# First inputs gathered in the router, down biases added in the last sums, the modulation product summed on VectorE

## The chip, the core and the metric

The kernel runs on one core of a Trainium2 chip. The metric is the device time of one execution, in microseconds (us). Matrix products run on TensorE (PE in the rows, its weight loads PEld), elementwise work on VectorE (DVE), ScalarE (ACT) and GpSimd (POOL); SyncE (SP) issues most DMAs, in its own order. Every engine works through its instructions in order.

## What is computed

512 tokens of width 1024 pass two layers of a first block (a gated linear recurrence, retention, spatial gating, a gated projection), then a second block: attention and a short convolution, both modulated, and a mixture of experts.

```
mod = silu(c) @ w_ada + b_ada            # 1024 -> 6 x 1024; a second row of it for the context
x = x + gt1 * (concat(attention, conv) @ w_out)
h2 = rmsnorm(x) * g_norm2 * (1 + sc2) + sh2
logits = h2 @ w_router + b_router        # 32 experts, the best 4 of each token, softmax gates
for each expert e, over its tokens:
    y = swiglu(h2[tok] @ w_gate_up[e] + b_gate_up[e]) @ w_down[e] + b_down[e]
    x[tok] += gt2 * gate * y
out = rmsnorm(x) * g_final
```

All data are float32. An expert's weights are 12 MB, all experts' 403 MB.

## The kernel before

**Dense stage** (`layer`, `block2`). Activations lie transposed, eight tiles `self.h` of 128 x 512. A weight is loaded into one of three buffers of the pool `wst` (tag `w`), split into a high part `wh` on ScalarE (L289) and a rest `wl` on VectorE (L290), and multiplied in three products (L284 to L286) of 128x128 by 128x512 into one of three PSUM banks `prj`. Up to three split weights are kept ready (`weights`, `next_weights`).

**Modulation** (`ada`, L773). 24 calls are strewn over the output projections, four in a stage of eight projections, after projections 0, 1, 4 and 5. A call loads two tiles `wa` of 512 KB into two of the same three `w` buffers. TensorE multiplies them by `sc`, the two conditioning columns padded to 32, in four products (L796), each in its own 32 columns of the array; every second call ScalarE copies the sum (L801), four small products with selector columns (L805) add up the four parts and turn them, and VectorE adds the bias (L807). Only the first eight calls hold columns that the context row needs.

**Router** (`router`, L1031). Beside the last output projection it turns `h` into rows `hr` (token by token), forms scaled rows `raw` (128 x 4 x 256, four of them, two in `wst` and two in the pool `late`) on GpSimd, logits, the four best experts (`mask`), the position `pos` of each token in its expert's list, and gates `G` into `vals`. Then `raw` is scaled by the norm and shifted: number 0 on ScalarE and GpSimd, 1 to 3 on VectorE (L1155), and stored by SP as `h_rows` (L1156), from which later experts gather tokens.

**Experts** (`moe`, L1757). `ORDER` lists two wide experts (0 and 1, 128 slots each), then narrow ones (64 slots, two weights halves at once in the array, L1588) and wide ones (L1549, L1550, down L1627) in turn. Weights stream through eight buffers of 1 MB in SP's order; a wide expert's are split on ScalarE and VectorE first (L289, L290). Experts 0 and 1 take their tokens by a product of `hr` with one-hot matrices `hots` (`first_slots`, `first_inputs`, L1428); the others by an indirect DMA from `h_rows` into `xg` or `xgn` (`slots`, L1502) and four transposes (L1518). Each expert's rows are added to `x_rows` in DRAM by an indirect DMA with an add (L1231).

Work beside an expert's products is a generator `work()`, one step per call of `fill`, four in each `gate_up`, two in `down`; what is left runs at the expert's end. From the second expert on each engine's order is the program's; before that a list scheduler orders by priority, and `high_priority(n)` moves an instruction ahead by n. `issue_after` and `behind` put an instruction behind another one in its engine's queue. In expert 0 the steps are: inputs of expert 1, `ranks` (the order of the experts by size), `slots(0, 0)` (indices and gates of 0 and 1) and `slots` of the first narrow pair; `slots` of the first wide pair comes in expert 1.

`residual` (L1310), in expert 0, forms down biases times gates: the bias tile `bst`, scaled on GpSimd and split into `gb`, the gates turned into `gT` (L1330), eight products (L1336), eight adds into `hr` (L1338), four stores to `x_rows` (L1339). `narrow_consts` copies positions and gates into `pg` for the picks of later slots (L1453). `expert_bias` splits the gate and up biases, the rest on VectorE (L1754). At the end the last two experts' rows are not added in DRAM: `finish_part` multiplies them by one-hot `to` into banks `fx` (L1690) and adds these to rows read back from `x_rows`.

## Time and profile before

| | |
|---|---|
| median of 3 runs | 2409.7 us (2406.43 to 2410.49) |
| the profiled execution | 2409.16 us, of which the span is 2407.0 us |
| TensorE busy | 2286.2 us, 95% of the span |
| VectorE busy | 1589.7 us, 66% |
| ScalarE busy | 982.7 us, 41% |
| GpSimd busy | 163.1 us, 7% |
| granted TensorE clock, mean | 0.986 of full speed |
| bytes moved by DMA | 563.59 MB, mean 234 GB/s |

The span has two parts: the dense stage and the router up to about 1265 us, and the experts after it. A busy share is an average over both and says little of either; the rows below are taken by stage.

### The profile page before, as it was taken

What the parts mean: (1) busy time and instruction counts of PE and PEld (TensorE: products, weight loads), DVE (VectorE), ACT (ScalarE), POOL (GpSimd) and SP (SyncE); (2) the same over time, 40 slices, a digit from 0 to 9 for tenths busy, and PEclk for the clock granted to TensorE, in tenths of its full rate; (3) what the DMA queues carried; (4) which work ended last, traced back from release to release, by engine and by line L of the source; (5) the groups of instructions that cost most, each with busy time, mean ns of one, the idle gap of its engine ahead of it and who ended that gap; (6) DMA issues with size and microseconds to landing.
All of it is one profiled execution on the core that took longest, in us unless ns stands there. A gap on an engine that the chain in (4) does not pass through costs nothing.

```text
span 2407.0 us, 29051 instructions
## 1 busy us (share of the span) xinstructions
PE 2286.2 (95%) x10863; PEld 1639.9 (68%) x10863; DVE 1589.7 (66%) x2487; ACT 982.7 (41%) x1166; POOL 163.1 (7%) x116
## 2 busy tenths in 40 slices
PE   8999999999999999999998789999999999999995
PEld 6778877777878878788876555555566555555552
DVE  8875764768747657786768856656666565656552
ACT  5632332435423324433455434334444443444421
POOL 0000000000000000000011111011111011011002
PEclk9999999999999999999998899999999999999998
DMA  4234334332342353422126689999999999999995
GB/s 163 86 112 122 99 117 129 125 118 86 94 151 88 99 164 109 142 74 83 55 88 236 251 337 401 407 395 403 395 401 392 403 397 400 403 396 404 412 399 227
DMA packets 109282, 563.59 MB, mean 234 GB/s; under 512 B 14440, under 2 KB 16872, under 8 KB 59984
## 3 DMA queue, kind: packets, MB, share of 16 engines
q1 hardware_dynamic: 95184, 532.33, 58.2%
q0 software_dynamic: 9200, 21.00, 3.2%
q10 hardware_dynamic: 4752, 8.36, 1.1%
q8 instruction: 87, 1.43, 0.2%
q14 instruction: 59, 0.48, 0.1%
HBM read 550.73 MB, written 18.87 MB: 237 GB/s over the span
## 4 chain that ended last, share of the span: by engine, by line
PE 81%; DMA 8%; DVE 7%; ACT 3%; issue 1%; POOL 0%; DVEq 0%; SPq 0%; ACTq 0%; POOLq 0%
PE prj L284 11%; PE prj L285 11%; PE prj L286 11%; PE pg L1549 7%; PE pd L1627 7%; PE pl L1550 7%; DMA w<-in_wgu 6%; PE pd L1650 4%; DVE wl L290 3%; PE pg L1588 2%; PE pl L1588 2%; ACT wh L289 2%; PE ada L796 1%; DMA w<-in_wdn 1%; PE cs L313 1%
## 5 line engine op out<-in xcount | busy, mean ns | idle before, releaser
L289 ACT ACTIVATE wh<-w 128x2048 fp32r<-128x2048 f32 (+3 forms) x382 | 560.4, 1469 | 587.2 <-PE prj L285 197.2
L290 DVE TENSOR_TENSOR wl<-w,wh 128x2048 fp32r<-128x2048 f32 (+3 forms) x382 | 660.2, 1734 | 205.3 <-ACT wh L289 204.8
L284 PE MATMUL prj<-ty,wh 128*128 128x512 f32 x880 | 353.0, 401 | 11.3 <-ACT wh L289 8.5
L285 PE MATMUL prj<-ty,wh 128*128 128x512 f32 x880 | 350.4, 398 | 1.2 <-DVE ty L823 0.9
L286 PE MATMUL prj<-ty,wl 128*128 128x512 f32 x880 | 349.7, 398 | 1.1 <-DVE wl L290 1.1
L1588 PE MATMUL pg<-w,xn 128*64 128x512 f32 x512 | 190.0, 600 | 39.4 <-DMA w<-in_wgu 39.3
L1549 PE MATMUL pg<-wh,x 128*128 128x512 f32 x512 | 210.1, 410 | 0.6 <-ACT wh L289 0.6
L1550 PE MATMUL pl<-wh,x 128*128 128x512 f32 x512 | 203.8, 398 | 0.0
L284 PEld LDWEIGHTS prj<-ty,wh 128*128 128x128 f32 x880 | 166.5, 189 | 50.4 <-ACT wh L289 10.6
L286 PEld LDWEIGHTS prj<-ty,wl 128*128 128x128 f32 x880 | 166.2, 189 | 41.1 <-DVE wl L290 2.4
L1569 DVE TENSOR_SCALAR li<-pl 128x512 f32<-128x512 f32 x48 | 33.0, 687 | 243.0 <-PE pl L1593 242.5
L285 PEld LDWEIGHTS prj<-ty,wh 128*128 128x128 f32 x880 | 166.4, 189 | 39.2 <-DVE ty L823 1.8
L1588 PE MATMUL pl<-w,xn 128*64 128x512 f32 x512 | 185.5, 595 | 0.0
L1568 ACT ACTIVATE sg<-pg 128x512 f32<-128x512 f32 x48 | 28.7, 597 | 308.6 <-PE pg L1593 260.8
L1588 PEld LDWEIGHTS pg<-w,xn 128*64 128x64 f32 x512 | 50.2, 136 | 125.2 <-DMA w<-in_wgu 69.7
L284 PE MATMUL prj<-tmix,wh 128*128 128x512 f32 x320 | 126.9, 398 | 0.3
L285 PE MATMUL prj<-tmix,wh 128*128 128x512 f32 x320 | 126.5, 395 | 0.0
L286 PE MATMUL prj<-tmix,wl 128*128 128x512 f32 x320 | 126.2, 395 | 0.0
L1650 PE MATMUL pd<-w,an 128*64 128x512 f32 x512 | 114.8, 596 | 7.6 <-DMA w<-in_wdn 6.1
L1549 PEld LDWEIGHTS pg<-wh,x 128*128 128x128 f32 x512 | 97.1, 190 | 32.5 <-issue 11.4
L1550 PEld LDWEIGHTS pl<-wh,x 128*128 128x128 f32 x512 | 97.3, 190 | 19.3
L1549 PE MATMUL pg<-wl,x 128*128 128x512 f32 x256 | 101.6, 397 | 0.4 <-DVE wl L290 0.4
(498 smaller groups left out, 3864.9 us busy)
## 6 DMA issues: line engine op xcount, KB each, us to landing
w<-in_wgu SPq DMA_DIRECT2D x256, 1024.0 KB, 12.6
w<-in_wdn SPq DMA_DIRECT2D x128, 1024.0 KB, 10.9
w<-in_w SPq DMA_DIRECT2D x118, 512.0 KB, 3.7
wa<-in_wada SPq DMA_DIRECT2D x48, 512.0 KB, 3.6
w<-in_wob SPq DMA_DIRECT2D x32, 384.0 KB, 3.1
w<-in_wg SPq DMA_DIRECT2D x16, 512.0 KB, 3.7
w<-in_wos SPq DMA_DIRECT2D x8, 512.0 KB, 3.6
w<-in_wo SPq DMA_DIRECT2D x8, 512.0 KB, 3.5
```

The source lines that it names most:

```text
L284: mm(ps, a[0], b[0], start=first, stop=False)
L285: mm(ps, a[0], b[1], start=False, stop=False)
L286: mm(ps, a[1], b[0], start=False, stop=last)
L289: ins = self.nc.scalar.activation(hi, src, AF.Copy).ins
L290: self.nc.vector.tensor_sub(lo, src, hi.bitcast(F32))
L1549: nc.tensor.matmul(pg, x[k], w[:, s, 0], start=first, stop=False)
L1550: nc.tensor.matmul(pl, x[k], w[:, s, 1], start=first, stop=False)
L1568: nc.scalar.activation(sg, pg, AF.Sigmoid, scale=1.702)
L1569: nc.vector.tensor_scalar(li, pl, 8.0, -6.0, op0=OP.min, op1=OP.max)
L1588: nc.tensor.matmul(p[64 * c:64 * c + 64], x[k], ws[c][:, s, h], start=k == 0, stop=False, skip_group_check=True)
L1627: nc.tensor.matmul(self.pd[n], a[:, k], w[:, s, n * 512:(n + 1) * 512], start=hf == 0 and k == 0 and a is ah and w is wh, stop=hf == 1 and ...
L1650: nc.tensor.matmul(pd[64 * n:64 * n + 64], a[:, k % 4, k // 4 * 64:k // 4 * 64 + 64], w[:, s, n * 512:(n + 1) * 512], start=k == 0, stop=k ...
```

## The change

- `ada`: the `wa` tiles stay as they are. VectorE multiplies each 512-column piece by the conditioning value of its partition and adds it to an accumulator of 128 x 512 (`adac`, and `rt` for the context row in the first eight calls), eight pieces to a sum; TensorE adds up the partitions by products with a column of ones. The padded `sc`, the ScalarE copy, the selector products and `onesm` go.
- `first_slots` and the first expert's `first_inputs` move into `router`, ahead of gates and counts, with banks of `prj` and a buffer of `mix`. `ranks` moves ahead of expert 0.
- `raw` 1 to 3 are scaled on ScalarE and shifted on GpSimd as 0 was; 2 and 3 queue behind the first expert's second input split on ScalarE. `hr` is stored to `x_rows` once, in the router.
- Slots of the first narrow and the first wide pair are both steps of expert 0; `slots(0, 0)` is one of expert 1.
- `residual` becomes `down_bias`, formed in the sixth expert of `ORDER`; its eight products start the sums in `finish_part`. The path for crowded experts, which does not run here, gets its own.
- `narrow_consts` and `pg` go: picks read `pos` and `vals` in three multiplications. The rest of the gate and up biases is formed on GpSimd.
- Pads shift the start of tiles that hold rows (`hr`, `xg`, `ye`, weights).

```
@@ ada
-            self.sc = self.small.tile([128, 8, 32], F32, name="sc", bufs=1)
+            self.sc = self.small.tile([128, 16], F32, name="sc", bufs=1)
+            self.adac = self.small.tile([128, T], F32, name="adac", bufs=1)
...
+        accs = [self.adac, self.rt][:2 if u < 4 else 1]
         for t in range(2):
             w = self.wst.tile([128, 1024], F32, name="wa", tag="w")
             nc.sync.dma_start(w, d["wada"][i, t])
-            ws.append(w)
-        for q in range(4):
-            nc.tensor.matmul(p[32 * q:32 * q + 32], self.sc[:, 4 * half + q], ws[q // 2][:, (q % 2) * 512:(q % 2) * 512 + 512],
-                             start=half == 0, stop=half == 1, skip_group_check=True)
+            for q in range(2):
+                k = 4 * half + 2 * t + q
+                for j, acc in enumerate(accs):
+                    c, x = self.sc[:, 2 * k + j:2 * k + j + 1], w[:, q * 512:q * 512 + 512]
+                    if k == 0:
+                        nc.vector.tensor_scalar(acc, x, c, None, op0=OP.mult)
+                    else:
+                        nc.vector.scalar_tensor_tensor(acc, x, c, acc, op0=OP.mult, op1=OP.add)
         if half == 0:
             return
-        m = self.tl("C")
-        nc.scalar.activation(m, p, AF.Copy)
...
+        for j, acc in enumerate(accs):
+            for b in range(4):
+                nc.tensor.matmul(p[:, 4 * j + b:4 * j + b + 1], acc[:, b * 128:(b + 1) * 128], self.ones, start=True, stop=True)
+            nc.vector.tensor_add(self.mod[:, j, u * 4:u * 4 + 4], p[:, 4 * j:4 * j + 4], self.cols[:, bo:bo + 4])
@@ router
         nc.vector.tensor_add(pos, pos, pc[:, :128].rearrange("p (b e) -> p b e", b=4))
+        self.xs = {}
+        with tc.high_priority(2 * AHEAD):
+            self.first_slots()
+            for _ in self.first_inputs(0, self.prj, lambda: self.tl("mix", F32)):
+                pass
...
+            with tc.high_priority(0 if j > 1 else AHEAD):
+                for b in range(4):
+                    with ExitStack() as c:
+                        if j > 1:
+                            c.enter_context(tc.issue_after(self.evicted[1]))
+                        nc.scalar.activation(r[:, b], r[:, b], AF.Copy, scale=nat[:, b:b + 1])
+                    if b % 2:
+                        nc.gpsimd.tensor_add(r[:, b - 1:b + 1], r[:, b - 1:b + 1], row[:, None].to_broadcast([128, 2, 256]))
             nc.sync.dma_start(self.h_d.rearrange("(b p) c -> p b c", p=128)[:, :, j * 256:j * 256 + 256], r)
+        nc.gpsimd.dma_start(self.x_d.rearrange("(b p) c -> p b c", p=128), self.hr)
@@ wsplit
-        with self.behind((self.hot,) if i == 0 else self.urgent if i < 8 else ()):
+        with self.behind(((self.hot, *self.evicted)[i],) if i < 3 else ()), self.tc.high_priority(AHEAD if i < 3 else 0):
             self.split(w, hi, lo)
@@ slots
-            nc.vector.tensor_mul(t, self.pg.rearrange("p c b e -> p (c b) e")[:, None].to_broadcast(S),
-                                 m[:, :, None, :].to_broadcast(S))
+            for j, x in enumerate((self.pos, v[:, :, :, 2], v[:, :, :, 3])):
+                nc.vector.tensor_mul(t[:, :, 4 * j:4 * j + 4], x[:, None].to_broadcast(S), m[:, :, None, :].to_broadcast(S))
@@ finish_part
+                    self.bias_product(self.fx[h, b], b, h, False)
@@ expert_bias
-                nc.vector.scalar_tensor_tensor(self.bias[r:r + 32], st[r:r + 32], one[r:r + 32],
-                                               self.bias[r:r + 32].bitcast(F32), op0=OP.add, op1=OP.subtract)
+            nc.gpsimd.tensor_add(st[r:r + 32], st[r:r + 32], one[r:r + 32].to_broadcast([32, 1024]))
+            nc.gpsimd.tensor_sub(lo, st[r:r + 32], lo.bitcast(F32))
@@ moe
+            pad(24)
             late = pool("mlate")
             self.work = late
+            pad(8)
...
-                    slots[max(before(p - 3 - 2 * (narrow and p > 6)), 1 - narrow)].append((r, narrow))
+                    slots[before(p - 3 - 2 * (narrow and p > 6))].append((r, narrow))
...
                     if p == 0:
-                        yield
-                        yield from self.first_inputs(1)
-                        self.ranks()
-                        yield
-                        yield
+                        yield from self.first_inputs(1, self.dn, lambda: self.early.tile([128, T], F32, name="x0", tag="sg"))
+                        self.hrow.close()
+                        self.xp = c.enter_context(tc.tile_pool(name="mx", bufs=1, reuse_waits="tile"))
+                    if p == 1:
                         yield from self.slots(0, 0)
...
-                    if t == 0 and hf == 1 and p == 0:
-                        with self.behind(self.urgent):
-                            self.residual()
-                            self.narrow_consts()
+                    if t == 0 and hf == 1 and p == 1:
+                        self.narrow_gain()
+                    if t == 0 and hf == 1 and p == 5:
+                        self.biases()
```

## Rows read from the trace of the kernel before

**Rows 1.** The chain that ended last, shares of the span by engine.

```profile
PE 81%; DMA 8%; DVE 7%; ACT 3%; issue 1%; POOL 0%; DVEq 0%; SPq 0%; ACTq 0%; POOLq 0%
```

**Rows 2.** Windows with ada: length; busy of PE, PEld, DVE, ACT, POOL; clock; DMA share; GB/s.

```profile
160.00:195.00 35.00, 34.78 (x160) 23.49 (x159) 14.98 (x21) 8.09 (x12) 0.00 (x0) 1.00 0.53 169
335.00:372.00 37.00, 37.00 (x173) 25.43 (x172) 23.47 (x76) 11.22 (x16) 0.10 (x1) 1.00 0.60 197
455.00:505.00 50.00, 50.00 (x243) 37.47 (x242) 26.88 (x46) 15.01 (x21) 0.00 (x0) 1.00 0.47 159
...
955.00:1005.00 50.00, 50.00 (x242) 37.30 (x241) 39.50 (x84) 25.74 (x45) 0.00 (x0) 1.00 0.43 142
```

**Rows 3.** Windows from the router's end: its tail, expert 0, expert 1, the rest.

```profile
1265.00:1295.00 30.00, 19.66 (x112) 16.77 (x110) 25.04 (x78) 13.23 (x20) 5.39 (x4) 0.72 0.55 197
1295.00:1337.00 42.00, 41.34 (x214) 33.49 (x213) 35.35 (x53) 26.07 (x26) 9.66 (x8) 1.00 0.80 298
1337.00:1404.00 67.00, 47.07 (x192) 36.25 (x191) 48.16 (x59) 28.16 (x23) 12.62 (x6) 0.82 0.70 259
1404.00:2380.00 976.00, 927.40 (x4177) 555.41 (x4175) 590.62 (x596) 390.81 (x312) 116.12 (x58) 1.00 0.99 396
```

**Rows 4.** Waits of PE before 1262 us, the longest: total us, times, longest one.

```profile
PE prj L284 <- ACT wh L289: 8.5, 4, 6.9
```

**Rows 5.** Groups by line: shapes, count, busy us, mean ns of one, idle before.

```profile
L313 PE MATMUL cs<-ones,tD 128*128 128x1 f32 x160 | 20.2, 244 | 0.3 <-ACT tD L1071 0.3
...
L504 DVE SCALAR_TENSOR_TENSOR tl<-tA,cols,tl 128x512 f32<-128x512 f32 x36 | 26.1, 744 | 0.3
...
L796 PE MATMUL ada<-wa,sc 128*32 128x512 f32 x192 | 33.9, 605 | 0.2 <-DMA wa<-in_wada 0.2
...
L805 PE MATMUL adat<-cols,tC 128*128 128x2 f32 x96 | 11.4, 240 | 0.0
```

**Rows 6.** Waits of PE from 1262 to 1405 us, the five longest.

```profile
PE xT L1518 <- DMA xg<-h_rows,si: 6.7, 1, 6.7
PE xT L1518 <- DMA xgn<-h_rows,sn: 6.5, 1, 6.5
PE slot L1477 <- DVE oh L1466: 4.1, 1, 4.1
PE xT L1428 <- DVE cnt L1144: 3.2, 1, 3.2
...
PE rb L331 <- DVE x L1432: 2.1, 1, 2.1
```

**Rows 7.** The chain in order of time in expert 1: start, us, what.

```profile
1369.69 5.62 PE pd L1627 x24
...
1398.91 4.51 PE pd L1627 x12
```

**Rows 8.** VectorE's instructions in order, router's tail and expert 0.

```profile
1281.98 3.25 DVE L1155 SCALAR_TENSOR_TENSOR tv<-tv,nat,tF 128x256 f32<-128x256 f32 x8
1285.26 1.27 DVE L1754 SCALAR_TENSOR_TENSOR bias<-bst,one,bias 32x1024 fp32r<-32x1024 f32 x1
...
1289.43 4.49 DVE L290 TENSOR_TENSOR wl<-w,wh 128x2048 fp32r<-128x2048 f32 x2
...
1308.09 3.15 DVE L290 TENSOR_TENSOR wl<-w,wh 128x2048 fp32r<-128x2048 f32 x1 [1.06 <-ACT wh L289]
```

**Rows 9.** GpSimd's instructions in order, the same stretch.

```profile
1273.83 2.58 POOL L1152 TENSOR_TENSOR raw<-raw,tF 128x512 f32<-128x512 f32 x2 [3.15 <-ACT raw L1150]
...
1304.98 4.11 POOL L1323 TENSOR_TENSOR gb<-bst,gb 32x512 fp32r<-32x512 f32 x2 [3.89 <-ACT gb L1322]
```

**Rows 10.** TensorE in the last sums, in order of time.

```profile
2382.35 3.07 PE L1690 MATMUL fx<-ys,to 64*128 64x512 f32 x23 [0.22 <-DVE ys L290]
```

**Rows 11.** DMA queues: packets, MB, share of 16 engines' span.

```profile
q1 hardware_dynamic: 95184, 532.33, 58.2%
q0 software_dynamic: 9200, 21.00, 3.2%
```

More of the change, by code (lines that the diff above doesn't have):

```diff
@@ L60 @@
 _reg("b_r", 1)
-_reg("sel2", 2)
 C_XL, C_GL, C_Q, C_K, C_V, C_G, C_U, C_VS, C_GS = 0, 6, 12, 18, 24, 30, 36, 40, 44
@@ L107, in prep @@
     col("b_r", np.concatenate([i["b_router_2"][0], np.zeros(96, f)]))
-    col("sel2", np.stack([(np.arange(128) % 32 == j).astype(f) for j in range(2)]))
     a["cols"] = cols
@@ L1194, in dense @@
             self.consts()
-            self.tri = self.small.tile([128, 128], F32, name="tri", bufs=1)
+            self.tri = late.tile([128, 128], F32, name="tri", bufs=1)
             nc.gpsimd.dma_start(self.tri, d["tri"])
@@ L1331, in residual, with bias_product, biases @@
         nc.scalar.activation(gt[:96], p[:96], AF.Copy)
[L1332 to L1341 removed]
+        return gt, gb
+    def bias_product(self, p, b, h, stop):
+        gt, gb = self.dbias
+        self.nc.tensor.matmul(p, gt[:96, b * 128:(b + 1) * 128], gb[:96, h * 512:h * 512 + 512], start=True, stop=stop)
+    def biases(self):
+        st = self.work.tile([128, D], F32, name="bst", tag="ye", bufs=2)
+        gb = self.early.tile([128, D + 24], F32R, name="gb", bufs=1)[:, :D]
+        gn = self.early.tile([128, T], F32, name="gn", tag="sg")[:, :384].rearrange("p (b m) -> p b m", b=4)
+        gt = self.work2.tile([128, T], F32R, name="gT", tag="gT")
+        self.dbias = self.down_bias(st, gb, gn, gt, self.g2, self.dn("gT"))
     def ranks(self):
@@ L1783, in moe @@
                 if r > 1 and (r - NW * narrow) % 2 == 0:
-                    slots[max(before(p - 3 - 2 * (narrow and p > 6)), 1 - narrow)].append((r, narrow))
-            for _ in self.first_inputs(0):
-                pass
-            self.urgent = self.hot, self.scaled
+                    slots[before(p - 3 - 2 * (narrow and p > 6))].append((r, narrow))
             act = down = None
-            self.split_next(3)
+            self.split_next()
+            with self.behind(self.evicted[:1]):
+                for b in range(4):
+                    self.first_slot(1, b)
+                self.ranks()
+            self.split_next(2)
             ordered = c.enter_context(ExitStack())
```

164 lines of the change are left out of this document (64 added, 100 removed).

## Prediction

> **What bounds the kernel now.** I read the chain of waits first: four fifths of it is TensorE [rows 1]. Then windows by stage, because the two parts have different limits. In the dense stage the windows show TensorE busy practically throughout, at the full clock, with DMA half idle [rows 2]; its longest wait before 1262 us is 8.5 us in four pieces, all for a split weight [rows 4]. So a microsecond taken from TensorE's queue there is a microsecond of the span, unless another engine takes its place, and VectorE is next: 15.0 of 35 us to 39.5 of 50 us [rows 2]. In the experts there are two regimes [rows 3]. After 1404 us the DMA engines are busy 0.99 of 976 us at 396 GB/s: this block has a fixed length and can only move as a whole. Before it, from 1265 to 1404 us, they are busy 0.55, 0.80 and 0.70, and TensorE stands idle 10.3 of 30 us and 19.9 of 67 us. The list of waits says for what: gathered rows (6.7 and 6.5), one-hots of a slot (4.1), a count copied out of a bank that the first inputs need (3.2), an input queued on VectorE (2.1) [rows 6].
>
> **The modulation.** Removed from TensorE: 33.9 us of products and 11.4 us of small ones [rows 5]. Added: 4 columns for each of 12 sums and a second accumulator in the first four, so 8 x 4 + 4 x 8 = 64 products with a column of ones. The 48 old small products stand as 96 records, so these are 128, at 20.2/160 = 0.126 us each from the same product in `colsum` [rows 5]: 16.2 us. Net 33.9 + 11.4 - 16.2 = 29.1 us less on TensorE.
>
> Added to VectorE: 24 calls of 4 pieces, 8 pieces in the first eight calls: 128 instructions. No row has this one (VectorE multiplies by a per-partition value and adds); the nearest is the convolution's, same form and size, 744 ns [rows 5]: 95 us. Stage by stage, four calls each (23.8 us in the first two stages, 11.9 us after). TensorE's relief is 4 x 1.41 + 1.9 less the new columns (4.0 or 2.0), so 3.5 and 5.5 us.
> First stage: VectorE 15.0 + 23.8 = 38.8 against TensorE 35 - 3.5 = 31.5, over by 7.3.
> Second: 23.5 + 23.8 = 47.3 against 33.5, over by 13.8.
> The one at 455 us: 26.9 + 11.9 = 38.8 against 44.5, it fits.
> The one at 955 us: 39.5 + 11.9 = 51.4 against 44.5, over by 6.9.
> All overflow together is 28 us. Nothing that TensorE needs soon reads the sums; they get in its way only by delaying VectorE's adds into `h`, for which three banks of `prj` give cover of two projections (some 8 us at the second stage's 33.5/8 = 4.2 us each), and by holding two of three `w` buffers longer. If the cover swallows everything the stage gains 29 us; if all overflow reaches TensorE, 1 us. I take 12 us of overflow as reaching it, somewhat under the middle, because one call's 6.0 us is inside the cover and only calls in succession exceed it: **-17 us**, ends -29 and -1.
>
> **The router's tail.** `first_inputs` with banks of its own no longer waits for the count (3.2 us), and the last eviction no longer queues behind splits (2.1 us; two `wl` of 4.49 us stood ahead) [rows 6, 8]: **-5 us**. VectorE loses 12 scalings (3.25 us for eight, so 4.9) and two bias rests of 1.27 us [rows 8]; GpSimd gets six additions of 1.29 us [rows 9] and four bias instructions of 32 rows x 1024. For the last the nearest row is 4.11 us for twice 32 x 512 with two inputs, so about 4 us each, 16 us, with 2 us below if they take half. They have until the end of the first half of `gate_up`, whose 48 products begin near 1290 and take 11 us at 0.234 us each [rows 7], with the other expert's inputs between them, so they cost nothing unless GpSimd's queue holds them behind rows 2 and 3 of `raw`.
> One row speaks against this move: a `wl` of the same shape takes 3.15 us at 1308.09, while a GpSimd subtraction runs, against 4.49 for two otherwise [rows 8, 9]. The stretch is about 0.9 us for 4.1 us of GpSimd. On 24 us of new GpSimd work that is 5 us of the 7.4 us that VectorE is spared. The Trainium skill says the same of it (SBUF — State Buffer, Who interferes with whom): a VectorE instruction with two SBUF inputs contends with a GpSimd instruction that reads SBUF. The trace agrees; by the rule and the row alike VectorE keeps 2 us of the relief.
>
> **Expert 0.** Eight products (L1336) leave TensorE, at 5.62/24 = 0.234 us each [rows 7]: **-2 us**. VectorE, busy 35.35 of 42 us [rows 3], loses eight additions into `hr` and the copies for `pg`; it gets the two slot chains. By the code these are near equal, so it stays near full; I charge 3 us for it below.
>
> **Expert 1.** The gathers for the narrow and wide pair were issued in this expert, too late; now the steps end with expert 0's second `down` tile, a whole expert before their use. The idle time of the window, 67 - 47.1 = 19.9 us [rows 3], goes. So does slow work: 12 products in 4.51 us where 24 took 5.62 us [rows 7] is 1.7 us lost. The granted clock of 0.82 over 67 us means 24 us at the lower level; at most 19.9 of these were idle, so 2 to 12 us were lost, and I take 4. Together 24; less the 3 us charged: **-21 us**. Next late would be weights: the DMA engines stood idle 13.5 + 8.4 + 20.1 = 42 us from 1265 to 1404 [rows 3], which is the ceiling of any shift there; 28 us is below it.
> Sum of experts: -5 - 2 - 21 = **-28 us**, ends -15 (half of the idle time returns as other waits) and -38 (12 us of clock, no charge).
>
> **What else moves.** The store of `x_rows` leaves expert 0's end for a queue slot in the router, where DMA has room. Loading `b_down` three times (0.4 MB) moves into the block that is bound by DMA: at 396 GB/s [rows 3] **+1 us**. The work on it runs beside the weights; ScalarE waits for the load and GpSimd's multiplication, estimated 4 us, while TensorE has up to three split tiles: nothing, ends 0 and +4. In the last sums eight products of about 0.23 us join; four fall into a wait for the last rows, four behind the products that the first half needs, while VectorE and ScalarE work on that half (TensorE has only 3.07 us left there [rows 10]): nothing, ends 0 and +1. Three multiplications for one in the picks: some 0.3 us on VectorE each, covered by the DMA bound. The pads change start addresses alone: the software queue takes 3.2% of 16 x 2407 us for 21.0 MB, 3.7 us per MB, the other queue 2.6 [rows 11]; if start addresses caused the difference, and they were mended, that is worth up to 22 us. I take 0: its packets are also smaller, 2.3 KB in the mean against 5.6, and no row ties the rest to addresses. The Trainium skill has another reason for slow adds (Collectives: The Full Stack, The bandwidth ceiling: the fold count and why AG ≠ RS ≠ AR): an add by DMA reads two sources. By that rule the pads give 0 and the sum stands; no row here separates the two.
>
> **Sum.** 2409.2 - 17 - 28 + 1 = **2365 us** against the profiled execution, which lies 0.5 us under the median of the runs. Its own range is 2346 to 2385.
>
> **Rivals.**
> A, VectorE becomes the bound of the ada stages: all 28 us of overflow reaches TensorE, the dense stage gains 1, total 2409.2 - 1 - 28 + 1 = 2381. For it: the second stage's 47.3 against 33.5. Against it: the windows between have room, and the sums are wanted late.
> B, a weight wait takes the place of the gather wait: SP issues in order, and it now stores `raw` 2 and 3 only after the second input split, eight ScalarE scalings and four GpSimd additions; weights queued behind them start late, TensorE meets DMA in expert 1, and half of the gain (13 us) is left: 2409.2 - 17 - 13 + 1 = 2380. For it: 42 us of DMA room is not much over 28.
> C, the pads do mend the adds: 15 to 22 us more, about 2347. Against it: the smaller packets explain a part, and nothing shows the rest.
> D, **slower**: the `wa` tiles hold two of three `w` buffers while VectorE adds, and the weight stream stops with them. Before, a call held TensorE 1.41 us; now a hold lasts 3.0 us, or 6.0 in the first eight calls. If every hold stops TensorE in full, that is 95 us, and the total 2409.2 + 95 - 29 - 28 + 1 = 2448. It decides against the change from (29 + 28)/24 = 2.4 us of stop per call. For it: the longest dense wait, 6.9 us, is already for a split weight [rows 4]. Against it: three split weights are ready, over 12 us of products.
> E, it does not do what it says: the list scheduler leaves slots and inputs where they were (these stretches have no fixed order) and VectorE eats the rest: within 5 us of 2409.
>
> **Chances.** Forecast 0.50, A 0.15, B 0.12, C 0.10, D 0.09, E 0.04. A difference of 0.2% (4.8 us) is about what a measurement can tell. Faster: the first four, 0.87; same: E, 0.04; slower: D, 0.09. The range takes in A, B and the near half of C and cuts off D, E and the tails of the forecast's ends: 2338 to 2392.
>
> **What would show it.** Right: no TensorE record of L796, some 128 VectorE records near 0.74 us in the ada windows, TensorE still busy there; the first L1549 product some 30 us of dense and router time earlier; no wait over 2 us for `xg`, `xgn` or `slot` in expert 1; a window from expert 0's first product to the narrow expert of some 85 us in place of 109; the DMA-bound block still 976 us long. Wrong: waits of `prj` products for `wh` or `wl` in the first two ada stages over 12 us (A, D); a wait for `w<-in_wgu` in expert 1 (B); a shorter DMA block with a cheaper q0 (C).

## The result, and the profile after

The changed kernel takes 2372.9 us (median of 4 runs, 2371.1 to 2374.6) against 2409.4 us (4 runs): a ratio of 0.985, interval 0.9833 to 0.9867, 36 us less. The forecast was 2365, some 44 us less, with a range of 2338 to 2392. The profiled execution, on which what follows rests, took 2374.6 us, of which the span is 2372.8.

One table carries the reading. It gives the start, in the trace of each kernel, of the router's last column sums (`cs`), of the first expert product, of the first product of four narrow experts, and the span.

| kernel | `cs` | first product | 1st narrow | 2nd | 4th | last narrow | span |
|---|---|---|---|---|---|---|---|
| before | 1268.2 | 1295.0 | 1404.2 | 1467.8 | 1598.0 | 2340.1 | 2407.0 |
| after | 1236.4 | 1266.0 | 1356.5 | 1422.1 | 1554.2 | 2304.7 | 2372.8 |
| gain | 31.8 | 29.0 | 47.7 | 45.7 | 43.8 | 35.4 | 34.2 |

So the total was near the forecast, but its parts were not. The dense stage gave 31.8 us where 17 were forecast; the router's tail lost 2.8 where 5 were to be won; experts 0 and 1 gave 18.7 (forecast 23, charge included); and from the first narrow expert on, where I had written that a block of fixed length moves as a whole, 12.3 us were given back.

The windows of after, in the columns of [rows 2, 3]: two with ada, then from the column sums to the first expert product, from there to the first narrow expert, and the block behind it.

```profile
160.00:195.00 35.00, 34.02 (x164) 27.89 (x163) 30.84 (x54) 7.31 (x10) 0.00 (x0) 1.00 0.52 165
335.00:372.00 37.00, 35.51 (x157) 29.41 (x156) 34.71 (x84) 8.52 (x11) 0.10 (x1) 0.91 0.55 169
...
1236.40:1266.00 29.60, 16.49 (x92) 14.40 (x93) 24.13 (x54) 8.61 (x18) 16.63 (x11) 0.65 0.64 248
1266.00:1356.50 90.50, 84.20 (x403) 67.94 (x401) 82.69 (x107) 59.41 (x57) 16.42 (x10) 0.94 0.76 285
1356.50:2344.60 988.10, 936.74 (x4180) 560.40 (x4179) 601.38 (x627) 392.52 (x314) 121.04 (x61) 0.98 0.98 394
```

In the ada windows VectorE carries 30.8 of 35 us and 34.7 of 37, where it carried 15.0 and 23.5 [rows 2]. Look at the clock column of the second: 0.91, where it was 1.00. The last line is the block: 988.1 us long, DMA busy 0.98 of it, where it was 976 us at 0.99 [rows 3]. Two things grew in it. It carries more bytes, 389.4 MB for 386.8, so the weights were less far ahead when it began: 2.6 MB are some 7 us at 394 GB/s. And the DMA engines had nothing to do for longer: 15.6 us for 7.9 by their packets, which the columns round to 0.02 and 0.01. The clock is 0.98 in it, where it was 1.00.

The chain still is TensorE's, with more of VectorE in it [rows 1]:

```profile
PE 76%; DVE 10%; DMA 9%; ACT 3%; issue 1%; ACTq 0%; DVEq 0%; POOLq 0%
```

The two longest waits of TensorE from the router's tail to the first narrow expert (total us, times, longest one):

```profile
PE xT L1418 <- DVE hots L1404: 7.8, 4, 3.8
PE cum L1114 <- DVE tE L1111: 3.7, 1, 3.7
...
```

These are the answer to [rows 6]. The gathers, the one-hots of a slot, the count and the queued input are gone, as forecast. In their place stand 7.8 us for the one-hots `hots`, which no part of the prediction names.

### The profile page after: what moved, and what is told of

Its sections match the earlier page's. It is cut to its first block, busy times and chain, and to the rows that moved or that the text cites. A ratio compares the mean times of both kernels' runs of the same rounds, so it can differ in the third digit from the quotient of the medians.

```text
span 2372.8 us, 28891 instructions
## 1 busy us (share of the span) xinstructions
PE 2257.6 (95%) x10703; PEld 1648.7 (69%) x10703; DVE 1674.7 (71%) x2623; ACT 983.3 (41%) x1166; POOL 174.6 (7%) x122
## 4 chain that ended last, share of the span: by engine, by line
PE 76%; DVE 10%; DMA 9%; ACT 3%; issue 1%; ACTq 0%; DVEq 0%; POOLq 0%
PE prj L282 9%; PE prj L283 9%; PE prj L284 9%; PE pg L1540 8%; PE pd L1618 7%; PE pl L1541 7%; DMA w<-in_wgu 6%; PE pd L1641 4%; DVE wl L288 3%; PE pg L1579 2%; PE pl L1579 2%; ACT wh L287 2%; PE vp L282 1%; DMA w<-in_wdn 1%; PE vp L283 1%
## 5 line engine op out<-in xcount | busy, mean ns | idle before, releaser
L282 PE MATMUL prj<-ty,wh 128*128 128x512 f32 x880 | 348.3, 396 | 10.8 <-ACT wh L287 8.1
L283 PE MATMUL prj<-ty,wh 128*128 128x512 f32 x880 | 346.8, 394 | 1.6 <-DVE ty L819 1.2
L1579 PE MATMUL pl<-w,xn 128*64 128x512 f32 x512 | 191.6, 616 | 0.0
L1579 PEld LDWEIGHTS pl<-w,xn 128*64 128x64 f32 x512 | 54.2, 141 | 73.1 <-issue 71.8
```

Of the source, the lines that this page charges most:

```text
L282: mm(ps, a[0], b[0], start=first, stop=False)
L283: mm(ps, a[0], b[1], start=False, stop=False)
L1579: nc.tensor.matmul(p[64 * c:64 * c + 64], x[k], ws[c][:, s, h], start=k == 0, stop=False, skip_group_check=True)
```

## The experiments

The same starts in their traces, in the order in which the runs are told:

| kernel | `cs` | first product | 1st narrow | 2nd | 4th | last narrow | span |
|---|---|---|---|---|---|---|---|
| modulation alone | 1246.3 | 1278.9 | 1390.3 | 1453.3 | 1583.5 | 2328.0 | 2394.8 |
| no pads | 1250.3 | 1279.8 | 1369.8 | 1435.5 | 1568.7 | 2318.3 | 2386.2 |
| half the accumulations | 1233.5 | 1263.5 | 1352.8 | 1418.1 | 1551.0 | 2297.7 | 2365.7 |
| double | 1301.1 | 1331.7 | 1422.1 | 1488.6 | 1621.7 | 2368.0 | 2437.9 |
| bias rest on VectorE | 1235.1 | 1262.0 | 1350.2 | 1414.4 | 1549.6 | 2294.0 | 2363.8 |
| one pick | 1235.8 | 1265.2 | 1355.2 | 1418.8 | 1554.9 | 2292.2 | 2359.6 |
| loads by GpSimd | 1236.8 | 1266.5 | 1357.0 | 1422.7 | 1561.5 | 2303.7 | 2372.3 |
| bias step in two | 1239.5 | 1266.4 | 1354.6 | 1418.7 | 1553.1 | 2291.6 | 2361.1 |
| rows stored by GpSimd | 1240.0 | 1267.1 | 1357.5 | 1421.9 | 1555.9 | 2293.5 | 2361.6 |
| slots put back | 1238.4 | 1268.7 | 1387.5 | 1452.8 | 1584.5 | 2329.0 | 2398.6 |
| bias rest behind the one-hot | 1240.3 | 1262.8 | 1354.5 | 1418.6 | 1553.0 | 2292.1 | 2359.9 |
| all rows behind the splits | 1235.2 | 1255.0 | 1350.5 | 1413.6 | 1546.6 | 2286.9 | 2354.5 |

**The modulation alone.** The kernel before with the new `ada`, and only what it needs (`sc`, `adac`, the longer `rt`, `tri` in another pool).

```
-            nc.tensor.matmul(p[32 * q:32 * q + 32], self.sc[:, 4 * half + q], ...)
...
+                        nc.vector.scalar_tensor_tensor(acc, x, c, acc, op0=OP.mult, op1=OP.add)
```

> The kernel before with the new modulation sum alone; router, experts and start addresses as before. Theory (the whole relief of TensorE arrives, VectorE's 91 us of new work are hidden): the last row sum of the router starts some 31 us earlier than before, at 1237, and since nothing behind it changes the whole 31 us are there at the end, about 2378. Rival (the overflow of VectorE in the first two modulation stages reaches TensorE, as forecast, and the rest of the 31.8 us came from another part of the change): 12 to 20 us earlier, end near 2392. Either way it tells what the router and expert parts gave at the end: changed kernel 2373 less this one.

Measured: 2400.0 us, ratio 0.9957 (0.9942 to 0.9971); `cs` at 1246.3, 21.9 us earlier. That lies between the two theories, nearer to the rival's 12 to 20. 21.9 of the dense stage's 31.8 us are the modulation's, and 10 come from another part. At the first product only 16.1 us of it are left, at the first narrow expert 13.9, at the last 12.1; the medians differ by 9.4. What took them, in the waits of TensorE from 1246 to 1391 us:

```profile
PE xT L1423 <- DVE x L1427: 7.6, 2, 6.7
PE xT L1513 <- DMA xg<-h_rows,si: 6.5, 1, 6.5
```

The list scheduler put an input of expert 1 behind other work on VectorE (7.6 us, where the wait for such an input was 2.1 [rows 6]), and the gathered rows are waited for as before. A gain ahead of a stretch that is ordered by a scheduler isn't handed on whole.

**The start addresses.** The changed kernel without its three pads.

```
-        c.tile([128, 16], F32, name="pad")
...
-            pad(24)
...
-            pad(8)
```

> The changed kernel without its three pads: the 64 bytes ahead of the dense tiles and the two ahead of the experts' pools. Theory S (the pads set where the operands of TensorE's products start, and aligned starts are read faster: the products of the dense stage follow each other every 227 ns in the changed kernel and every 231 ns in the kernel before and with the new modulation sum alone): 231 ns again, the router's last row sum 8 to 10 us later, near 1245, and the end 5 to 10 us later, 2378 to 2383. Rival (the order of instructions gave these 10 us): 227 ns, no change. Rival C of the prediction (starts decide what an add by DMA costs): the software queue's time per MB rises from the changed kernel's 3.7 us.

Measured: 2385.7 us, ratio 0.9895 (0.9879 to 0.9912); `cs` at 1250.3. The products of the dense stage by the tiles they read, after (minimum, median and maximum duration in ns, first and last start):

```profile
L282 PE MATMUL prj<-ty,wh x880: 387/389/792, 6.7 to 1134.7; 128*128 128x512 f32 x176
...
L282 PE MATMUL prj<-tmix,wh x320: 387/389/735, 159.4 to 1233.9; 128*128 128x512 f32 x160
```

and without the pads:

```profile
L282 PE MATMUL prj<-ty,wh x880: 387/394/793, 6.7 to 1148.6; 128*128 128x512 f32 x176
...
L282 PE MATMUL prj<-tmix,wh x320: 388/389/735, 162.3 to 1247.9; 128*128 128x512 f32 x160
```

Products that stream `ty` fall from a median of 394 ns to 389; those that stream `tmix` have 389 either way. Their spacing says it more sharply: an unbroken run of 121 products takes 27.20 us from the first start to the last in the changed kernel (51.84 to 79.04), 226.7 ns each, and 28.00 us, 233.3 ns each, without pads, in the kernel before (52.31 to 80.31) and with the modulation alone. 2640 products at 6.6 ns are 17 us at most; 9.9 (against the modulation alone) and 13.9 (against this kernel) were seen at `cs`. Part of the 13.9 is the clock: without pads it stood at its lower level for 27 us of the dense stage, in the changed kernel for 14, which is some 7 us of work. Theory S holds, at some 10 us. Rival C of the prediction falls: the software queue's share of 16 engines is 3.3% for 21.00 MB with and without pads, 3.3% of 2372.8 us over 21.00 MB = 3.7 us per MB as before [rows 11].

```profile
q0 software_dynamic: 9152, 21.00, 3.3%
```

**Less and more VectorE work.** First the context row's sum left out, then every accumulation done twice.

```
-        accs = [self.adac, self.rt][:2 if u < 4 else 1]
+        accs = [self.adac]
...
```

> The changed kernel, but the sum for the context row is left out in the first eight calls, and its modulation is taken from the other row's sum; VectorE's work in the first two modulation stages is halved, 23.8 to 11.9 us each, and TensorE loses 16 column products a stage (2.0 us). Theory A or D in small (in the second stage, where the changed kernel gained nothing, VectorE's overflow or the held buffers ate TensorE's relief): beyond 2.0 us of columns each, the second stage is another 4 to 6 us shorter, the first at most 2. Rival (the second stage gained nothing for another reason): 2 us in each and no more, router 4 us earlier in all.

```
...
                         nc.vector.scalar_tensor_tensor(acc, x, c, acc, op0=OP.mult, op1=OP.add)
+                    nc.vector.scalar_tensor_tensor(acc, x, self.zero, acc, op0=OP.mult, op1=OP.add)
```

> The changed kernel with each accumulation of the modulation repeated with a factor of zero, 128 instructions of 0.745 us more on VectorE (95 us), nothing else; the sums stay the same. By the same sum as in the prediction VectorE's overflow over TensorE, stage by stage, grows from 28 to some 95 us. If overflow is only lent (three banks and the stretches between the calls swallow it, as the changed kernel suggests: 7 of 28 us arrived), a quarter, some 17 us of the 67 new ones, arrives and the router's last row sum stands near 1254. If beyond the cover all of it arrives, 50 us and more, 1287 or later, with TensorE's waits for a split or a banked sum in the first two modulation stages.

Measured: with half the work in the first two stages 2367.1 us (2 runs), `cs` at 1233.5, 2.9 us earlier, all of it no more than the 4.0 us of columns. From the 881st to the 1201st product into `prj`, which holds the second stage, 84.1 us pass, 86.7 in the changed kernel: 2.6 less, of which 2.0 are columns. The rival holds, as far as it can be told beside the 5 us named below; VectorE's overflow cost that stage nothing that shows. With the double work: 2439.7 us (one run), `cs` at 1301.1, 64.7 us later. Not all of it is the work: with the added tile `zero` the spacing of the products is back at 233.3 ns (120 products from 51.69 to 79.45 us, ahead of the first call), and this is their row:

```profile
L282 PE MATMUL prj<-ty,wh x880: 387/396/796, 6.9 to 1199.1; 128*128 128x512 f32 x176
```

So the fair comparison is with the two kernels of the same spacing: `cs` is 54.8 us later than with the modulation alone and 50.8 later than without pads, of 67 by the sum. Its waits of TensorE in the dense stage, and two windows:

```profile
PE prj L282 <- ACT wh L287: 15.8, 8, 6.9
PE ada L806 <- DVE adac L799: 10.4, 6, 4.0
PE ada L806 <- DVE rt L799: 5.8, 4, 2.1
```

```profile
160.00:230.00 70.00, 59.20 (x242) 47.69 (x241) 62.44 (x103) 12.81 (x17) 0.00 (x0) 0.88 0.42 130
370.00:470.00 100.00, 88.37 (x358) 71.34 (x359) 76.03 (x119) 23.47 (x29) 0.31 (x3) 0.86 0.37 113
```

So the cover was there, and was used up: of 28 us of overflow at most 7 arrived, of the next 67 some 51 to 55. But not as waits alone: in the two windows TensorE stands 10.8 and 11.6 us, and a clock of 0.88 and 0.86 costs up to another 8.4 and 14.0 us of work. The clock was not in the sum. The window row of the modulation alone at its second stage:

```profile
335.00:372.00 37.00, 35.81 (x152) 30.03 (x151) 34.03 (x90) 7.33 (x10) 0.10 (x1) 0.86 0.51 156
```

A clock of 0.86 over 37 us is 10.4 us at the lower level (1.2 of 2.4 GHz), 5 us of work lost; in the changed kernel 0.91 is 6.7 us, 3.3 lost. Before the change it was 1.00 [rows 2]. In the changed kernel the clock is 1.00 up to 355 us and 0.80 from 355 to 372; TensorE had stood 1.3 us for a sum ahead of the column product at 352.62 us. Whether that wait or the short column products beside it go with the fall, these runs don't separate. Kernels whose dense stage is the changed kernel's differ by up to 5 us at `cs`, 1235.1 to 1240.3 in eight of them.

**Where the bias rest is formed.** On VectorE, meant to stand behind the second input split.

```
-            nc.gpsimd.tensor_add(st[r:r + 32], st[r:r + 32], one[r:r + 32].to_broadcast([32, 1024]))
-            nc.gpsimd.tensor_sub(lo, st[r:r + 32], lo.bitcast(F32))
...
+                nc.vector.scalar_tensor_tensor(self.bias[r:r + 32], st[r:r + 32], one[r:r + 32],
+                                               self.bias[r:r + 32].bitcast(F32), op0=OP.add, op1=OP.subtract)
```

> The changed kernel, but the rest of the gate and up biases is formed on VectorE behind the first expert's second input split (two instructions near 1.27 us), not on GpSimd. Theory G (each of the four one-hots stood on VectorE until a GpSimd instruction ended: 8.4 us for four, where four alone take 1.4): the one-hots take under 2 us together, the first expert product starts 6 to 7 us earlier after the router's last row sum, 23 us in place of 29.7. At the end 3 to 7 us of it are left if the weight stream starts earlier with it, 0 if the weights set the pace from there. Rival (the one-hots wait for something else, positions or the norm): still 8 us and no change.

Measured: 2367.7 us, ratio 0.9832 (0.9813 to 0.9851). First what the one-hots were up against: VectorE in the router of the changed kernel, in order,

```profile
1243.35 1.36 DVE L1132 TENSOR_TENSOR tE<-tB,mx 128x128 f32<-128x128 f32 x1
1244.63 1.28 DVE L1119 TENSOR_SCALAR pos<-tE 128x128 f32<-128x128 f32 x1
...
1247.57 8.39 DVE L1404 TENSOR_SCALAR hots<-rt,pos,nat 128x128 f32<-128x128 f32 x4
```

and GpSimd in the same stretch:

```profile
1242.02 5.03 POOL L1156 TENSOR_TENSOR raw<-raw,tF 128x512 f32<-128x512 f32 x4 [2.40 <-ACT raw L1154]
1247.13 3.92 POOL L1748 TENSOR_TENSOR bst<-bst,one 32x1024 f32<-32x1024 f32 x2
1251.12 4.75 POOL L1749 TENSOR_TENSOR bias<-bst,bias 32x1024 fp32r<-32x1024 f32 x2
```

`tE` and `pos` keep the step of the additions to `raw`, 1.26 us each; the four one-hots end with the four bias instructions (1.96 and 2.38 us each), the last at 1255.96 where GpSimd ends at 1255.87. For each of these six, one of GpSimd's passes. The three instructions between them (0.27, 0.27 and 0.18 us from 1247.14 on) run at their own length beside the first bias instruction. With the bias rest on VectorE the four one-hots are this row:

```profile
1249.58 1.11 DVE L1404 TENSOR_SCALAR hots<-rt,pos,nat 128x128 f32<-128x128 f32 x4
```

7.3 us less, theory G as written. The first product comes only 2.8 us earlier after `cs` (26.9 for 29.7), where 6 to 7 were expected: the list scheduler ran the bias rest ahead of the router's norm and not behind the split. The Trainium skill has this (SBUF — State Buffer, Who interferes with whom): a per-partition scalar operation or copy in VectorE's two-port mode and a GpSimd instruction take the shared port pair in turn, for the whole instruction. The trace agrees for the one-hots, 2.1 us for one that alone takes 0.34.

**One pick multiplication.**

```
-            for j, x in enumerate((self.pos, v[:, :, :, 2], v[:, :, :, 3])):
-                nc.vector.tensor_mul(t[:, :, 4 * j:4 * j + 4], x[:, None].to_broadcast(S), m[:, :, None, :].to_broadcast(S))
...
+                nc.vector.tensor_mul(t, self.pg.rearrange("p c b e -> p (c b) e")[:, None].to_broadcast(S),
+                                     m[:, :, None, :].to_broadcast(S))
```

> The changed kernel, but from the second expert on the picks read a packed copy of positions and gates in one multiplication, as before the change, in place of three (0.96 us in place of 1.68). Theory P (the three multiplications hold back the VectorE split that frees a weight buffer, so the weight stream stops some 0.7 us more for each pair of experts): the loss of 8.4 us between the fifth and the last narrow expert goes, end near 2365. Rival L (the lead that TensorE won ran ahead of the DMA stream and had to be given back, whatever VectorE does): end within 2 us of the changed kernel, 2373, and the same loss from pair to pair.

Measured: 2364.5 us, ratio 0.9822 (0.9806 to 0.9839). The picks in the changed kernel, and here (minimum, median, maximum ns):

```profile
L1445 DVE TENSOR_TENSOR pick<-vals,rm x30: 597/607/680, 1274.8 to 2123.9; 128x256 f32<-128x256 f32 x30
L1445 DVE TENSOR_TENSOR pick<-pos,rm x15: 418/425/426, 1274.3 to 2123.1; 128x256 f32<-128x256 f32 x15
```

```profile
L1455 DVE TENSOR_TENSOR pick<-pg,rm x13: 957/957/961, 1385.1 to 2113.0; 128x768 f32<-128x768 f32 x13
```

Two of 607 ns and one of 425 against one of 957: 0.68 us more for each of 13 slot steps, 8.9 us in all. By the tables the changed kernel fell from 43.8 us ahead of before at the fourth narrow expert to 35.4 at the last; this one rose from 43.1 to 47.9. The two traces differ more than the kernels do: the one of the changed kernel is its slowest execution, this one its fastest, and the medians are 8.4 us apart, at the 2365 that theory P forecast. Of the twelve kernels that have the changed kernel's experts none mixes the sign: with three multiplications 0.1 to 8.4 us are lost there (seven kernels), with one 1.8 to 4.8 are won (five). Over the whole block, from the first narrow expert to the last, three multiplications lose 5.6 to 12.6 us and one 0.1 to 1.7. So theory P holds in its size, and rival L, by which the lead is lost whatever VectorE does, falls.

The way is another matter. SP's waits from the fourth narrow expert to the last (total us, times, longest one), in the changed kernel (1554.2 to 2304.7 us) and here (1554.9 to 2292.2):

```profile
SPq L1241 <- DVE wl L288: 398.7, 119, 8.4
SPq L1241 <- PE pl L1579: 129.3, 64, 6.3
```

```profile
SPq L1241 <- DVE wl L288: 399.4, 119, 8.4
SPq L1241 <- PE pl L1590: 116.3, 62, 4.4
```

The wait for the split that frees a weight buffer, the way that theory P names, is the same. What grew is the wait for the narrow products that free the other buffers: over the same stretch 121.0 to 130.1 us in the seven kernels and 116.3 to 119.2 in the five. How 0.68 us of VectorE a step reach those products stays open; the clock's part (20.5 us at the lower level there in the changed kernel, none here) is not separated.

**The sixth expert.** Two ways to mend the 8 us that the changed kernel stood there. First the loads on another queue:

```
-            nc.sync.dma_start(st[r:r + 32], self.d["bdn"])
+            nc.gpsimd.dma_start(st[r:r + 32], self.d["bdn"])
```

> The changed kernel, but the three loads of the down biases are issued by GpSimd, not by SP, so that SP's weight queue doesn't stand behind them until their buffer is free (10.5 us in the sixth expert). Theory: the 4.2 us that the changed kernel lost from the sixth expert on (its lead over the kernel before fell from 48.0 to 43.7 us there) stay, end near 2369. Rival L (the lead is lost to the DMA stream in any case): the lead falls to 43 us within the next pairs all the same, end 2373.

Measured: 2375.9 us, ratio 0.9865 (0.9849 to 0.9882): not better. The lead fell further, from 45.1 us at the second narrow expert to 36.5 at the fourth. TensorE's wait for `gn` is still there, 4.4 us, with SP free: SP's wait was not its cause. A new wait of 4.9 us came beside it: the loads land later, GpSimd's multiplication with them (1483.23 us), and ScalarE stands 14.8 us for that ahead of an input split. A wait of TensorE in the block of the changed kernel, and VectorE in its order at that place, say what was:

```profile
PE gT L1326 <- DVE gn L1324: 5.6, 1, 5.6
```

```profile
1470.19 3.53 DVE L288 TENSOR_TENSOR wl<-w,wh 128x2048 fp32r<-128x2048 f32 x1 [2.85 <-ACT wh L287]
1473.64 0.62 DVE L1324 COPY gn<-vals 128x128 f32<-128x128 f32 x3
```

The copies `gn` stand behind a split that itself waits 2.85 us for ScalarE and takes 3.5 us beside GpSimd's multiplication; with the loads by GpSimd it takes 2.3, so the stretch is only 1.2 of the 5.6 us. TensorE's fixed order holds everything behind the four transposes of `gn`. So the step was cut in two, with the pick and the bias rest of the two versions above:

```
...
                     if t == 0 and hf == 1 and p == 5:
-                        self.biases()
+                        self.bsteps = self.biases()
+                        next(self.bsteps)
+                    if t == 2 and hf == 1 and p == 5:
+                        next(self.bsteps, None)
```

> The changed kernel with one pick multiplication, the bias rest on VectorE, and the forming of the down biases cut in two: loads, gain and copies in the step where all of it stood, ScalarE's split and the four transposes two weight tiles later. If the loss in the sixth expert (the lead over the kernel before fell by 8 us and half came back) is TensorE standing in its fixed order behind copies that are queued behind a split, it falls by under 3 us; then the lead is near 54 us at the first narrow expert, 52 after, and the end is near 2358. If SP's wait for the buffer is the cause, the loss stays, and the end is near 2361.

Measured: 2364.0 us, ratio 0.9812 (0.9796 to 0.9829). The stall is gone: the third narrow expert starts at 1485.7 us, 47.5 us ahead of before (1533.2), where the changed kernel has 39.5 (1493.7). But at the first the lead is 49.6 and at the fourth 44.9, where 54 and 52 were expected, and the end is at 2364 and not near 2358. Between the first and the fourth 4.7 us go, 3.9 in the changed kernel with its stall: so far rival L was right. TensorE won 136.0 - 120.1 = 15.9 us between `cs` and the first narrow expert; the DMA engines stood idle there for 10.7 + 21.7 = 32.4 us (29.6 x 0.36 and 90.5 x 0.24 of the windows above) in place of some 40 (42 from 1265 us on [rows 3], 3 us ahead of `cs`). So the weights had followed by some 8 us of the 15.9, and the rest is caught up by the fourth: this kernel moves 77.6 MB between the first and the fourth, the kernel before 74.9. But it is not lost for good: at the last narrow expert the lead is 48.5 of the 49.6 us again. What gives it back is open.

**Rows 2 and 3 stored by GpSimd.**

```
+            eng = nc.gpsimd if j > 1 else nc.sync
...
```

> The last one, with rows 2 and 3 of the scaled rows stored by GpSimd and not by SP. Rival B of the prediction in small (SP, in order, stands 24 us behind the sums of these rows, and the weights behind it come late): up to 8 us of DMA idle time in the 60 us after the router go and the end comes 3 to 8 us earlier. If the weight buffers were full at that time anyway: within 2 us of the last one.

Measured: 2365.0 us, ratio 0.9816 (0.98 to 0.9833), the same as the last. Rival B's queue was there and cost nothing that shows: SP's waits for the sums of these rows fall from 22.1 to 6.5 us, but SP then stands 19.6 us at a later instruction, and the DMA engines are idle 29.2 us between `cs` and the first narrow expert, 26.8 in the last version.

**The slot steps put back.**

```
-                    slots[before(p - 3 - 2 * (narrow and p > 6))].append((r, narrow))
+                    slots[max(before(p - 3 - 2 * (narrow and p > 6)), 1 - narrow)].append((r, narrow))
...
```

> The changed kernel with the slot steps where they were: slots of the first wide pair in the second expert, those of experts 0 and 1 in the first. Theory (the window from the first product to the first narrow expert shrank by 18.7 us because the gathers are issued a whole expert before their use): waits for gathered rows of 5 us and more are back in the second expert, the first narrow expert starts 12 to 18 us later, and the end is 8 to 12 us later, near 2382, because the DMA engines stand idle so much longer there. Rival (DMA has caught up by the sixth expert whatever happens before): the first narrow expert later, but the end within 3 us of 2373.

Measured: 2397.9 us, ratio 0.9951 (0.9936 to 0.9966), 25 us more than the changed kernel, where 8 to 12 were expected. The waits are back, as in [rows 6], and longer; below them the two windows from `cs` on:

```profile
PE xT L1509 <- DMA xgn<-h_rows,sn: 11.1, 1, 11.1
PE xT L1509 <- DMA xg<-h_rows,si: 9.4, 1, 9.4
```

```profile
1238.40:1268.70 30.30, 17.58 (x94) 15.26 (x94) 23.81 (x54) 8.63 (x18) 15.65 (x10) 0.61 0.63 243
1268.70:1387.50 118.80, 88.40 (x400) 70.68 (x399) 87.04 (x107) 59.71 (x56) 21.72 (x11) 0.84 0.65 236
```

The windows from `cs` to the first narrow expert are 29.0 us longer than with the change, and the DMA engines stand idle for 11.2 + 41.6 = 52.8 us there, 20 more than the 32.4. At the last narrow expert 24.3 us are left, 22.3 without the 2.0 by which `cs` is later, about as much as the DMA engines lost; the rival falls.

**Towards a faster version.** The bias rest behind the fourth one-hot; then rows 0 and 1 of `raw` too behind the input splits.

```
-        with self.behind(self.evicted[1:]):
+        with self.behind((self.hot,)):
```

> The version with one pick multiplication and the down biases cut in two, with the bias rest on VectorE put behind the fourth one-hot (in the two versions before it ran ahead of the router's norm and held that for 2.5 us). First expert product 24 to 25 us after the router's last row sum in place of 26.9; end 2 us earlier than that version, ratio near 0.980; 0 us earlier if the weights set the pace from there.

```
...
-                        if j > 1:
-                            c.enter_context(tc.issue_after(self.evicted[1]))
+                        c.enter_context(tc.issue_after(self.evicted[j // 2]))
```

> The last one, with rows 0 and 1 of the scaled rows also put behind the first expert's input splits, so that no GpSimd addition runs while VectorE forms mask, positions and one-hots. Theory G: the VectorE instructions of 1.25 to 1.36 us there fall to 0.3, and the first expert product comes another 3 to 4 us earlier, 21 us after the last row sum. Rival: the rows' stores come later, SP stands behind them, and the weights queued there come late: the end is not earlier, or up to 6 us later.

Measured: 2361.6 us, ratio 0.9799 (0.9785 to 0.9813), first product 22.5 us after `cs`; and 2361.3 us, 0.9801 (0.9787 to 0.9814), 19.7 us after. Both beat before and changed kernel; against each other they are even, as the rival of the second had it. VectorE in the router of the second, and GpSimd:

```profile
1242.11 0.28 DVE L1132 TENSOR_TENSOR tE<-tB,mx 128x128 f32<-128x128 f32 x1
1242.31 0.22 DVE L1119 TENSOR_SCALAR pos<-tE 128x128 f32<-128x128 f32 x1
...
1243.79 1.11 DVE L1413 TENSOR_SCALAR hots<-rt,pos,nat 128x128 f32<-128x128 f32 x4
...
1258.46 1.35 DVE L1353 TENSOR_TENSOR key<-cnt,rt 128x128 f32<-128x128 f32 x1
...
1261.03 1.20 DVE L1464 CAST rvals<-tok 128x16 fp32r<-128x16 f32 x1
```

```profile
1255.46 2.53 POOL L1155 TENSOR_TENSOR raw<-raw,tF 128x512 f32<-128x512 f32 x2 [16.04 <-ACT raw L1153]
1257.96 3.01 POOL L1155 TENSOR_TENSOR tv<-tv,tF 128x512 f32<-128x512 f32 x2
1260.92 1.28 POOL L1155 TENSOR_TENSOR raw<-raw,tF 128x512 f32<-128x512 f32 x1
```

Mask, positions and the four one-hots run undisturbed, 0.28, 0.22 and 1.11 us. The cost has moved, not gone: the same GpSimd additions now stretch `key` and `rvals` of the ranks to 1.35 and 1.20 us, and the first narrow expert comes 115.3 us after `cs`, with 114.2 in the version before.

## Why the prediction was right in sign and size, and wrong in its parts

The forecast was a gain of 44 us, and 36 came. The mechanisms of the two large terms were right; three prices were wrong (the pads, the router's tail, the picks in the block), and the errors cancel. That the total came within 8 us is luck.

**The modulation** was mis-sized on the safe side: -17, measured -21.9. The groups agree with the sum: 91.5 us on VectorE where 95 were forecast, 16.0 us of column products where 16.2 were.

```profile
L796 DVE SCALAR_TENSOR_TENSOR adac<-wa,sc,adac 128x512 f32<-128x512 f32 x84 | 62.9, 748 | 2.5 <-DMA wa<-in_wada 1.5
...
L796 DVE SCALAR_TENSOR_TENSOR rt<-wa,sc,rt 128x512 f32<-128x512 f32 x28 | 20.9, 745 | 0.0
...
L794 DVE TENSOR_SCALAR adac<-wa,sc 128x512 f32<-128x512 f32 x12 | 5.8, 485 | 10.2 <-DMA wa<-in_wada 10.1
...
L794 DVE TENSOR_SCALAR rt<-wa,sc 128x512 f32<-128x512 f32 x4 | 1.9, 482 | 0.0
```

```profile
L803 PE MATMUL ada<-ones,adac 128*128 128x1 f32 x96 | 11.8, 244 | 5.2 <-DVE adac L796 3.0 <-DVE rt L302 2.1
...
L803 PE MATMUL ada<-ones,rt 128*128 128x1 f32 x32 | 4.2, 252 | 0.1
```

What failed is "I take 12 us of overflow as reaching it". No wait for a split grew (8.1 us for 8.5). "Nothing that TensorE needs soon reads the sums" failed too: the column products stand 5.2 us for them (the row above), 5.9 with half the work in the first two stages and 16.2 with the double, so at this size it goes with their place in the order more than with the amount. Two windows, from the start to `cs`, say where the missing 7 of 29.1 us are, before and with the modulation alone:

```profile
0.00:1268.20 1268.20, 1248.17 (x6155) 996.35 (x6155) 878.36 (x1667) 517.10 (x770) 14.12 (x36) 1.00 0.35 110
0.00:1246.30 1246.30, 1219.19 (x5995) 999.47 (x5995) 953.11 (x1798) 512.45 (x758) 13.89 (x35) 0.99 0.36 111
```

TensorE stands 27.1 us for 20.0, and after the first 20 us the clock is at its lower level for 13.7 us for 6.8, some 3 us of work more. The cover was larger than I took it for, and its end is near: doubled work broke through it. Rivals A and D fall for this size of work. The sum of the overflow was also too small: it left out the stage at 840 us,

```profile
840.00:870.00 30.00, 30.00 (x140) 21.33 (x139) 20.80 (x67) 8.36 (x12) 0.00 (x0) 1.00 0.57 179
```

where 20.8 + 11.9 = 32.7 on VectorE stand against 30 - 5.5 = 24.5 on TensorE: 8.2 us more, 36 in all.

**The pads**, "I take 0", is the step that failed outright. It weighed start addresses only for the software queue, where nothing changed, and never asked which engine reads the shifted tiles most often. TensorE does: some 10 us in the dense stage. The list of the change names only tiles that hold rows; the first pad, of 64 bytes, stands ahead of the dense tiles.

**The router's tail** was -5 and came out +2.8. The count and the queued input did go. But the cost of GpSimd work was taken from one row, 0.9 us of stretch for 4.1 us of GpSimd [rows 8, 9], and set against VectorE's spare time. The row was misread: the GpSimd pair ends at 1309.09 us and the split begins at 1308.09, so they share 1.0 us, not 4.1, and nearly all of it is stretch. The short instructions of the router's tail each waited in the same way for most of a GpSimd instruction, and these stood on the path. Mis-sized: 7 us for the one-hots, and mask and positions on top.

**Experts 0 and 1** were right: no wait for `xg`, `xgn` or `slot` above 2 us; the window from the first product to the first narrow expert 90.5 us, where some 85 were forecast and 109 stood before. The step that carries it, the moved slots, is worth 25 us at the end by itself. The ends given for the experts' term don't follow from their own words (about -18 and -39 for -15 and -38); nothing else rests on them.

**The block** "has a fixed length and can only move as a whole": this step is wrong. The block took 988 us for 976. What is lost in it goes with three multiplications where the prediction wrote "some 0.3 us on VectorE each, covered by the DMA bound". They are 0.68 us, and not covered: 12.3 us from the first narrow expert to the last in the changed kernel's trace, 0.1 to 1.7 in the five kernels with one, and 8.4 us between the medians. A lead that DMA had not followed can explain the 3.9 us up to the fourth narrow expert, but the kernels with one multiplication win theirs back. DMA busy 0.99 of a block doesn't mean that work beside it is free.

**The small terms**: the last sums' products and the loads of `b_down` are within +1.2 us together (the span behind the last narrow expert's start, 66.9 and 68.1). The forming of the down biases, priced at 0 to +4, stood for up to 8 us and cost little at the end: the kernel with one pick has the same stall and loses 1.1 us over the whole block, the version without it 1.1 too.

Sum of the measured parts: -31.8 + 2.8 - 18.7 + 12.3 + 1.2 = -34.2 us of span.

## What to carry to other kernels

A stretch at 99% of DMA doesn't cover every small thing beside it: count what is added to an engine in each round, times the rounds, and time it alone before calling it covered. Before work goes to GpSimd, look at which VectorE instructions run beside it: if they are short and on the path, each may wait for a GpSimd instruction's end, so place the work beside something that nobody waits for. And when tiles move in memory, compare the spacing of the products that read them.

## What the runs showed of the hardware

- The same 128x512 product in a dense run follows its predecessor after 226.7 ns with 64 bytes of pad ahead of its streamed tile and after 233.3 without, some 10 us of the dense stage; a small tile added elsewhere (`zero`) brought 233.3 back. Which property of the start it is these runs don't tell apart.
- Beside GpSimd, VectorE's mask, positions and one-hots, 0.2 to 0.34 us by themselves, take 1.3 to 2.5 us: they end with the GpSimd instruction that runs. Not all do: three of 0.27, 0.27 and 0.18 us passed beside one undisturbed.
- In the second modulation stage, where the clock was 1.00 before, TensorE waited 0.9 to 1.8 us for a sum in all twelve kernels with the new modulation at single or half work, and 3 to 10 us at the clock's lower level followed. In the changed kernel the wait is 1.3 us and the lower level 6.8, 3.4 us of work. That the wait is the cause is not shown.
